# Routing stage of a two-block layer: the order on VectorE and ScalarE written out by hand, the sums of squares and the late bf16 splits moved behind the index chain, one quarter of the output projection emitted in two halves

## The chip, the cores and the metric

The kernel runs on one core of a Trainium2 chip. The metric is device time in microseconds (us) of one execution. The kernel before took 942.03 us (median of 3 runs, 939.92 to 942.48).

## The reference, cut to what matters

Two transformer blocks follow each other on 256 tokens of width 1024. The change lies at the end of the second block, where its output projection is added to the residual and the tokens are routed to 32 experts (4 groups of 8, the best group and the best 2 of its experts):

```python
mix = jnp.concatenate([y_a, y_b], axis=-1)
x = x + jnp.einsum('bse,ed->bsd', mix, w_out[l])
h = rmsnorm(x, ffn_norm[l]).reshape(B * S, D)
...
group_logits = jnp.einsum('td,dg->tg', h, w_group)
g_sel = jnp.argmax(group_logits, axis=-1)
expert_logits = jnp.einsum('td,de->te', h, w_router)
...
in_prob = jax.nn.softmax(in_group, axis=-1)
top_p, top_i = lax.top_k(in_prob, EXPERT_TOPK)
...
hid = silu(h @ w_gate[e]) * (h @ w_up[e]) * combine[..., e]
y = y + hid @ w_down[e]
```

## The kernel before, in words

**Projection.** The output projection `w_out_2` is the generator `tm_steps`. It runs over four quarters of the inner dimension in the order `WO = [0, 2, 1, 3]`, and each quarter multiplies two token tiles `t` by two column halves `c` into four PSUM tiles `ps_wo` (`acc[t][c]`). Every product is three matmuls (high by high, low by high, high by low). The weights of the last quarter are split ahead of time into the tiles `hph` and `hpl`; its 24 matmuls (4 tiles x 2 inner steps x 3) come last, tile after tile. The generator is advanced by `next(wo)`, and `step` advances the attention work that is emitted between.

**Routing.** `route` handles four blocks `(t, c)` of 128 tokens by 512 columns. For each block VectorE adds the projection to the residual (`w<-w,ps_wo`), TensorE transposes the sum (four `ps_acc<-ident,w`), VectorE or ScalarE (ACT) copies the transposed block to `h3T`, and TensorE makes the router logits from it (`ps_acc<-wgr,h3T`). Each block is also split into three bf16 parts in the tiles `h3` (rows name them `h`): ACT rounds the sum (`h<-w`), VectorE takes the remainder (`r_rem<-w,h`), ACT rounds that (`h<-r_rem`), VectorE takes the last remainder (`h<-r_rem,h`). ACT also makes the sum of squares of each block (`r_ss`) for the norm. From the logits VectorE makes the choice of experts in some twenty small instructions (from `rm` to `rM`), TensorE counts positions with a triangular matrix (`lt`), VectorE writes `posm`, and from it the 0/1 matrices `Gm` that gather the tokens of four experts. The norm factors (`r_sm`, `r`) come from a chain of tiny VectorE instructions over `r_ss`.

**Experts.** `experts` then runs on TensorE in an order written out by hand: the gather (`ps_acc<-Gm,h`, 24 short matmuls for the first half), the copies `xg` out of PSUM by ACT and VectorE in turns, the up products (`ps_acc<-w,xg`), the down products (`ps_acc<-w,mhT`) and the scatter into `ps_wo` (`Y`). Weights stream in through a ring of 1 MB tiles `w` from the SP queue; a load waits until its tile has been given free. One of these tiles is the residual itself (`w_87` when numbered), free once routing has read it.

**What sets the order.** Each engine runs its own queue in order. In `route` the order on every engine is found by a list scheduler, with a priority offset (`high_priority(offset=RP[t])`) for the adds, transposes and copies; TensorE is by hand only in `experts`. Small temporaries of `route` live in a pool that is closed before `experts` opens its own pool in the same memory.

Of the kernel before, what the change touches and what calls it, by code (L numbers as in the profile page):

```python
# [6 lines left out]
F32 = mybir.dt.float32  # L7
# [62 lines left out]
MP = 2  # L70
MS = {mybir.EngineType.DVE, mybir.EngineType.Activation, mybir.EngineType.PE}
# [21 lines left out]
class K:  # L93
# [362 lines left out]
    def tm_steps(self, src, x, nk, xt=(), tag="acc", pre=(), order=None, each=None):  # L456
# [13 lines left out]
        for n, r in enumerate(order):  # L470
# [9 lines left out]
            for t in range(2):  # L480
                for k, w in now:
                    for c in range(2):
                        mms(k, t, c, w)
                    if each:
                        each()
            yield acc
# [1096 lines left out]
    def block2(self):  # L1583
# [170 lines left out]
        wo = self.tm_steps(a["w_out_2"], mx, 8, xt, "wo", [self.tload(a["w_out_2"], r) for r in WO], WO, lambda: step(NW))  # L1754
        more = True
        for n, r in enumerate(WO):
# [16 lines left out]
            if n < 3:  # L1773
                next(wo)
                step(NS)
        for self.acc2 in wo:
            pass
# [14 lines left out]
    def route(self, big, wgr):  # L1792
# [8 lines left out]
        self.rs3, sums = [], []  # L1801
        CS = [slice(c * 512, (c + 1) * 512) for c in range(2)]
        for t in range(2):
            ts = slice(t * 128, (t + 1) * 128)
            h = self.hres[t]
            ss = pool.tile([128, 2], F32, name="r_ss", bufs=2)
            sums.append(ss)
            with self.tc.high_priority(offset=RP[t]):
                for c in range(2):
                    self.tt(h[:, CS[c]], h[:, CS[c]], acc[t][c], OP.add)  # L1810
                    p = self.ps("acc")
                    for k in range(4):
                        self.tr(p[:, k * 128:(k + 1) * 128], h[:, (4 * c + k) * 128:(4 * c + k + 1) * 128])
                    dst, src = hT[:, 4 * c:4 * c + 4, ts], p.rearrange("p (a b) -> p a b", a=4)
                    V.tensor_copy(dst, src) if RE[2 * t + c] else self.cpa(dst, src)
            with self.tc.high_priority(offset=RQ[t]):
                for k in range(8):
                    self.mm(lg[:, t], hT[:, k, ts], wgr[:, k, :], k == 0, k == 7)
            self.dump_rows("x2", t, h)
        for t in range(2):  # L1820
            for c in range(2):
                self.act(h3[2][:, t, CS[c]], self.hres[t][:, CS[c]], AF.Square, accum_out=sums[t][:, c:c + 1])
        for t in range(2):
            for c in range(2):
                src = self.hres[t][:, c * 512:(c + 1) * 512].rearrange("q (p k) -> q k p", k=8)
                b = [x[:, t].rearrange("q (k p) -> q k p", k=8)[:, :, 64 * c:64 * c + 64] for x in h3]
                r = big.tile([128, 8, 64], F32, name="r_rem", bufs=2)
                e1, e2 = [(V, self.G)[x] for x in SE[4 * t + 2 * c:4 * t + 2 * c + 2]]
                self.cpa(b[0], src)
                self.tt(r, src, b[0], OP.subtract, eng=e1)  # L1830
                self.cpa(b[1], r)
                self.tt(b[2], r, b[1], OP.subtract, eng=e2)
        self.Y = [[self.ps("wo") for _ in range(2)] for _ in range(2)]
        for t in range(2):
            for c in range(2):
                self.mm(self.Y[t][c], self.ident, self.hres[t][:, CS[c]], True, False)
# [17 lines left out]
        o1 = first_max(el, m1, "r1", [4, 8], more8)  # L1854
        in2 = mb("rin2", 4, 8)
        self.stt(in2, o1, -3.0e38, el, OP.mult, OP.add)
        first_max(gl, gm, "rg", [4], more4[:, :8], ohg)
        ogb = ohg[:, :, :, None].to_broadcast([128, 2, 4, 8])
# [308 lines left out]
```

## Time and profile before

| | before |
|---|---|
| median of 3 runs | 942.03 us |
| profiled execution, its own time | 944.24 us |
| span of that execution, first to last instruction | 942.5 us |
| TensorE busy, and mean granted clock | 885.3 us (94%), 0.961 of full speed |
| VectorE (DVE), ACT, GpSimd (POOL) busy | 596.3, 413.3, 48.1 us |
| weights and data moved | 197.56 MB, mean 210 GB/s |

The profiled execution took 1.7 us more than its span, and 2.2 us more than the median of the runs. Busy shares are means over stages; the stage of the change is 679 to 700 us from the span's start, and the experts take the time from there on. A busy TensorE is not one at its peak, since ends of matmuls are modelled.

### The profile page before, as it was taken

What the parts mean: (1) busy time and instruction counts of PE and PEld (TensorE: products, weight loads), DVE (VectorE), ACT (ScalarE), POOL (GpSimd) and SP (SyncE); (2) the same over time, 40 slices, a digit from 0 to 9 for tenths busy, and PEclk for the clock granted to TensorE, in tenths of its full rate; (3) what the DMA queues carried; (4) which work ended last, traced back from release to release, by engine and by line L of the source; (5) the groups of instructions that cost most, each with busy time, mean ns of one, the idle gap of its engine ahead of it and who ended that gap; (6) DMA issues with size and microseconds to landing.
All of it is one profiled execution on the core that took longest, in us unless ns stands there. A gap on an engine that the chain in (4) does not pass through costs nothing.

```text
span 942.5 us, 15955 instructions
## 1 busy us (share of the span) xinstructions
PE 885.3 (94%) x6204; PEld 671.2 (71%) x6204; DVE 596.3 (63%) x1477; ACT 413.3 (44%) x807; POOL 48.1 (5%) x73
## 2 busy tenths in 40 slices
PE   7986989999999999999998999999989999999983
PEld 6986867689999899998877998886654443444421
DVE  6698699979888667665578788666473222323214
ACT  4373335376855246654452456576452111222102
POOL 2000232111000000000000010000000000000001
PEclk7898789999999999999999999999999999999997
DMA  6624222134696356646772543334969999999971
GB/s 186 186 69 142 82 90 90 57 123 136 199 293 216 97 180 181 188 170 229 254 234 87 179 134 109 117 134 145 388 239 347 374 396 398 410 404 408 406 258 48
DMA packets 111028, 197.56 MB, mean 210 GB/s; under 512 B 13161, under 2 KB 77906, under 8 KB 110946
## 3 DMA queue, kind: packets, MB, share of 16 engines
q1 hardware_dynamic: 110658, 195.95, 60.1%
q8 instruction: 51, 0.84, 0.4%
q10 hardware_dynamic: 288, 0.52, 0.1%
q14 instruction: 31, 0.25, 0.1%
HBM read 195.40 MB, written 1.05 MB: 208 GB/s over the span
## 4 chain that ended last, share of the span: by engine, by line
PE 72%; DVE 15%; ACT 6%; DMA 4%; issue 2%; POOL 0%; SPq 0%; DVEq 0%; ACTq 0%
PE ps_acc L132 41%; PE ps_mm L132 25%; PE ps_wo L132 4%; DVE wlo L139 3%; PE ps_acc L136 2%; ACT whi L154 2%; DMA w<-in_w_up_dram 2%; DVE cv_y L148 1%; DVE s5z L807 1%; DMA w<-in_w_down_dram 1%; DVE s5z L139 1%; ACT mo_P L151 1%; DMA ln_g<-in_ln_g_dram 1%; DVE r L148 1%; DMA w<-in_w_in_dram 1%
## 5 line engine op out<-in xcount | busy, mean ns | idle before, releaser
L139 DVE TENSOR_TENSOR wlo<-w,whi 128x1024 fp32r<-128x1024 f32 x150 | 185.6, 1240 | 77.6 <-ACT whi L154 76.7
L154 ACT ACTIVATE whi<-w 128x1024 fp32r<-128x1024 f32 x150 | 158.2, 1058 | 167.0 <-PE ps_mm L132 110.1
L132 PE MATMUL ps_mm<-hph,whi 128*128 128x256 f32 x424 | 122.7, 289 | 0.0
L132 PE MATMUL ps_mm<-hph,wlo 128*128 128x256 f32 x424 | 121.3, 286 | 0.0
L132 PE MATMUL ps_mm<-hpl,whi 128*128 128x256 f32 x424 | 121.0, 285 | 0.0
L132 PE MATMUL ps_acc<-w,xg 128*64 128x512 f32 x512 | 117.0, 597 | 0.0
L132 PE MATMUL ps_mm<-hTh,wlo 128*128 128x256 f32 (+1 forms) x360 | 107.0, 297 | 7.2 <-DVE pre L866 6.2
L132 PE MATMUL ps_mm<-hTh,whi 128*128 128x256 f32 (+1 forms) x360 | 108.8, 303 | 0.7 <-ACT gth L151 0.4
L132 PE MATMUL ps_mm<-hTl,whi 128*128 128x256 f32 (+1 forms) x360 | 106.2, 295 | 0.0
L132 PEld LDWEIGHTS ps_acc<-w,xg 128*64 128x64 f32 x512 | 35.2, 137 | 67.7 <-issue 62.5
L132 PEld LDWEIGHTS ps_mm<-hph,whi 128*128 128x128 f32 x424 | 80.5, 190 | 1.8 <-issue 1.8
L132 PEld LDWEIGHTS ps_mm<-hph,wlo 128*128 128x128 f32 x424 | 80.4, 190 | 1.2 <-issue 1.2
L132 PEld LDWEIGHTS ps_mm<-hpl,whi 128*128 128x128 f32 x424 | 80.5, 190 | 0.6 <-issue 0.6
L132 PEld LDWEIGHTS ps_mm<-hTh,wlo 128*128 128x128 f32 x360 | 72.0, 200 | 8.5 <-DVE pre L866 6.4
L132 PEld LDWEIGHTS ps_mm<-hTh,whi 128*128 128x128 f32 x360 | 72.1, 201 | 6.0 <-issue 2.6
L132 PEld LDWEIGHTS ps_mm<-hTl,whi 128*128 128x128 f32 x360 | 71.8, 200 | 0.8 <-issue 0.7
L132 PE MATMUL ps_acc<-w,mhT 128*32 128x512 f32 x512 | 59.4, 594 | 1.0 <-DVE mhT L1991 1.0
L151 ACT ACTIVATE mth<-ps_acc,cb 128x256 f32<-128x256 f32 x16 | 7.6, 474 | 119.8 <-PE ps_acc L132 119.8
L148 DVE SCALAR_TENSOR_TENSOR mth<-mth,ps_acc 128x256 f32<-128x256 f32 x16 | 6.7, 420 | 82.5 <-ACT mth L151 82.5
L139 DVE TENSOR_TENSOR hpl<-ps_acc,hph 128x512 fp32r<-128x512 f32 x40 | 26.0, 685 | 49.8 <-ACT hph L154 49.8
L154 ACT ACTIVATE hph<-ps_acc 128x512 fp32r<-128x512 f32 (+1 forms) x44 | 23.7, 576 | 62.6 <-PE ps_acc L132 61.7
L132 PEld LDWEIGHTS ps_acc<-w,mhT 128*32 128x32 f32 x512 | 19.6, 110 | 34.3 <-issue 30.0
(605 smaller groups left out, 1732.5 us busy)
## 6 DMA issues: line engine op xcount, KB each, us to landing
w<-in_w_down_dram SPq DMA_DIRECT2D x46, 1024.0 KB, 6.7
w<-in_w_in_dram SPq DMA_DIRECT2D x36, 1024.0 KB, 5.3
w<-in_w_gate_dram SPq DMA_DIRECT2D x60, 512.0 KB, 10.9
w<-in_w_up_dram SPq DMA_DIRECT2D x60, 512.0 KB, 10.0
w<-in_w_up_dram SPq DMA_DIRECT2D x16, 1024.0 KB, 5.8
w<-in_m_w_out_dram SPq DMA_DIRECT2D x4, 1024.0 KB, 5.6
w<-in_s_w_glu_dram SPq DMA_DIRECT2D x8, 512.0 KB, 5.8
w<-in_w_o_dram SPq DMA_DIRECT2D x4, 1024.0 KB
```

The source lines that it names most:

```text
L132: self.PE.matmul(out, lhsT, rhs, start=start, stop=stop, **kw)
L136: self.PE.transpose(out, in_, self.ident[:n, :n])
L139: (eng or self.V).tensor_tensor(out, a, b, op)
L148: (eng or self.V).scalar_tensor_tensor(out, a, s, b, op0, op1, **kw)
L151: self.S.activation(out, in_, func, bias=bias, scale=scale, **kw)
L154: self.S.activation(out, in_, AF.Copy)
L807: self.V.tensor_tensor_scan(flat(z[:, i]), d, flat(z[:, i]), 0.0, OP.mult, OP.add)
```

## The change

`tm_steps` gets a parameter `mid`: in quarter number 2 it yields once more after the first token tile, and the caller takes one more `next`. In `route` the loops over the blocks are replaced by a sequence of calls inside `manual_schedule(engines=RM)`, which holds the written order on VectorE and ACT (TensorE is still ordered by the scheduler). The priorities are gone. Per block there are now `add` (add and transposes), `logits`, `first`, `second` and `third` (the steps of the split). The sums of squares stand last and write their unused output to `hT` (rows: `h3T`) instead of `h3`.

```diff
+RM = {mybir.EngineType.DVE, mybir.EngineType.Activation}
...
+                if n == mid and t == 0:
+                    yield acc
...
-            with self.tc.high_priority(offset=RP[t]):
-                for c in range(2):
-                    self.tt(h[:, CS[c]], h[:, CS[c]], acc[t][c], OP.add)
-                    p = self.ps("acc")
-                    for k in range(4):
-                        self.tr(p[:, k * 128:(k + 1) * 128], h[:, (4 * c + k) * 128:(4 * c + k + 1) * 128])
...
-        for t in range(2):
-            for c in range(2):
-                self.act(h3[2][:, t, CS[c]], self.hres[t][:, CS[c]], AF.Square, accum_out=sums[t][:, c:c + 1])
...
+        def first(t, c):
+            src, b = part(t, c)
+            self.cpa(b[0], src)
+
+        def second(t, c):
+            src, b = part(t, c)
+            rem[t, c] = r = big.tile([128, 8, 64], F32, name="r_rem", bufs=2)
+            self.tt(r, src, b[0], OP.subtract)
+            self.cpa(b[1], r)
+
+        def third(t, c):
+            src, b = part(t, c)
+            self.tt(b[2], rem[t, c], b[1], OP.subtract)
...
+        with self.tc.manual_schedule(engines=RM):
+            dst, src = add(0, 0)
+            first(0, 0)
+            V.tensor_copy(dst, src)
+            logits(0, 0)
+            dst, src = add(0, 1)
+            second(0, 0)
+            self.cpa(dst, src)
+            logits(0, 1)
+            first(0, 1)
+            dst, src = add(1, 0)
+            third(0, 0)
+            first(1, 0)
+            V.tensor_copy(dst, src)
+            logits(1, 0)
+            dst, src = add(1, 1)
+            first(1, 1)
+            second(0, 1)
+            V.tensor_copy(dst, src)
+            logits(1, 1)
+            third(0, 1)
+            second(1, 0)
...
+            self.mm(p[:, 0:64], self.lt, Mf.rearrange("p t e -> p (t e)"), True, True)
+            second(1, 1)
+            third(1, 0)
+            third(1, 1)
+            self.stt(self.posm, p[:, 0:64], 1.0, Mff.bitcast(F32), OP.add, OP.mult)
+            for t in range(2):
+                for c in range(2):
+                    self.act(hT[:, 4 * c:4 * c + 4, t * 128:(t + 1) * 128],
+                             self.hres[t][:, CS[c]].rearrange("p (a b) -> p a b", a=4), AF.Square,
+                             accum_out=sums[t][:, c:c + 1])
```

TensorE, in the last quarter of the projection, before: matmul 10 of its 24, then the transposes of the first block, then the others with the second block's transposes among them.

```order
L132 MATMUL ps_wo<-hph,mx2h 128x512
L136 MATMUL ps_acc<-ident,w 128x128 x4
L132 MATMUL ps_wo<-hpl,mx2h 128x512
L132 MATMUL ps_wo<-hph,mx2l 128x512
L132 MATMUL ps_wo<-hph,mx2h 128x512
L132 MATMUL ps_wo<-hpl,mx2h 128x512
L132 MATMUL ps_wo<-hph,mx2l 128x512
L132 MATMUL ps_wo<-hph,mx2h 128x512
L132 MATMUL ps_wo<-hpl,mx2h 128x512
L136 MATMUL ps_acc<-ident,w 128x128 x4
```

The same engine after: the last of the 24 projection matmuls, and what follows it.

```order
L133 MATMUL ps_wo<-hph,mx2l 128x512
L137 MATMUL ps_acc<-ident,w 128x128 x4
L133 MATMUL ps_wo<-w,ident 128x512
L133 MATMUL ps_acc<-wgr,h3T 128x36 x4
L137 MATMUL ps_acc<-ident,w 128x128 x4
L133 MATMUL ps_wo<-w,ident 128x512
L137 MATMUL ps_acc<-ident,w 128x128 x3
L133 MATMUL ps_acc<-wgr,h3T 128x36 x4
L137 MATMUL ps_acc<-ident,w 128x128
```

All transposes have moved behind the 24 matmuls, and the logits of each block stand between them; the three transposes of the third block are parted from the fourth by the logits of the second.

ACT in `route`, before: the squares are the rows that write `r_ss`.

```order
L151 ACTIVATE h_7679,r_ss<-w 128x512
L154 ACTIVATE h_7679<-w 128x8x64
L151 ACTIVATE h_7679,r_ss<-w 128x512
L154 ACTIVATE h_7679<-r_rem 128x8x64
L154 ACTIVATE h3T<-ps_acc 128x4x128
L154 ACTIVATE h_7679<-w 128x8x64
L151 ACTIVATE h_7679,r_ss<-w 128x512
L154 ACTIVATE h_7679<-w 128x8x64
L151 ACTIVATE h_7679,r_ss<-w 128x512
```

ACT at the same place after, up to the first exponentials of the router (`re`).

```order
L155 ACTIVATE h_7679<-w 128x8x64
L155 ACTIVATE h_7679<-r_rem 128x8x64
L155 ACTIVATE h3T<-ps_acc 128x4x128
L155 ACTIVATE h_7679<-w 128x8x64 x3
L155 ACTIVATE h_7679<-r_rem 128x8x64 x3
L152 ACTIVATE h3T,r_ss<-w 128x4x128 x4
L152 ACTIVATE re_7850<-re_7850,r_7824 128x4
```

The four squares have moved behind all eight roundings.

VectorE from the end of the choice (`rM`) to the first `Gm`, after, with the engines that each row waits for (before, seven rows stand between `rM` and `Gm`, `posm` and small ones, none of them longer than 128x64 elements and none waiting for ACT).

```order
L140 TENSOR_TENSOR rM<-ro_7786,ro_7787 128x64 [waits DVE_49]
L140 TENSOR_TENSOR r_rem<-w,h_7679 128x512
L140 TENSOR_TENSOR h_7679<-r_rem,h_7679 128x8x64 [waits Activation_49] x2
L149 SCALAR_TENSOR_TENSOR posm<-ps_acc,rM 128x64 [waits PE_49]
L140 TENSOR_TENSOR r_sm<-r_ss 128x1 [waits Activation_49]
...
L149 SCALAR_TENSOR_TENSOR r_7824<-r_7825,r_7824 128x1 [waits DVE_49]
L140 TENSOR_TENSOR Gm<-iota_343,posm 128x128 [waits Activation_49]
```

One remainder and two last remainders now stand between `rM` and `posm`, and `Gm` waits for ACT, since its memory lies in the closed pool that the squares write; the sum `r_sm` of the second token tile, a few rows later, has no wait of its own.

## Rows read from the trace of the kernel before

**Rows 1.** The page, part 4: shares of the span in the chain of work that ended last, by engine.

```profile
PE 72%; DVE 15%; ACT 6%; DMA 4%; issue 2%; POOL 0%; SPq 0%; DVEq 0%; ACTq 0%
```

**Rows 2.** The chain that ended last, in order of time, from the last projection quarter on: start in us from the span's start, length, engine, tile written, line, count.

```profile
679.49 4.01 PE ps_wo L132 x10
...
684.14 0.50 DVE h3T L1815
...
687.62 1.05 ACT h L154
...
691.41 2.07 ACT h L154 x3
693.50 1.08 DVE r_rem L139
...
698.60 0.22 DVE posm L148
...
699.23 16.31 PE ps_acc L132 x109
...
897.49 1.13 PE ps_wo L132 x4
```

**Rows 3.** The list of waits from 690 to 942 (who waited for whom: us in total, times, longest), and one stretch of the experts from the view by stretches (busy us of PE, PEld, DVE, ACT and POOL with their counts, granted clock, mean share of the DMA engines, GB/s).

```profile
PEld ps_acc L132 <- DMA w<-in_w_up_dram: 0.7, 3, 0.3
...
PEld ps_acc L132 <- DMA w<-in_w_gate_dram: 0.3, 1, 0.3
...
740.00:760.00 20.00, 20.00 (x167) 8.87 (x165) 6.57 (x19) 4.93 (x10) 0.00 (x0) 1.00 1.02 407
```

**Rows 4.** The timeline of the last projection quarter: start us, us, engine, line, operation, out<-in, count, in brackets the idle time before and who ended it.

```profile
681.83 0.69 DVE L139 TENSOR_TENSOR w<-w,ps_wo 128x512 f32<-128x512 f32 x1 [1.54 <-PE ps_wo L132]
...
682.87 0.63 PE L132 MATMUL ps_wo<-hph,mx2h 128*128 128x512 f32 x1
...
683.30 0.80 PE L136 MATMUL ps_acc<-ident,w 128*128 128x128 f32 x4
...
684.40 0.39 PE L132 MATMUL ps_wo<-hph,mx2h 128*128 128x512 f32 x1
...
684.63 0.39 PE L132 MATMUL ps_wo<-hpl,mx2h 128*128 128x512 f32 x1
...
684.75 0.68 DVE L139 TENSOR_TENSOR w<-w,ps_wo 128x512 f32<-128x512 f32 x1
...
685.34 1.13 DVE L139 TENSOR_TENSOR r_rem<-w,h 128x512 f32<-128x512 f32 x1
...
685.55 0.60 PE L136 MATMUL ps_acc<-ident,w 128*128 128x128 f32 x4
```

**Rows 5.** The timeline further on: a square with the read of its accumulator and the rounding behind it, the copy to `h3T` on ACT, a second rounding, two last remainders on VectorE.

```profile
688.55 0.64 ACT L151 ACTIVATE h<-w 128x512 bf16<-128x512 f32 x1
...
689.08 0.21 ACT L151 ACTIVATION_READ_ACCUMULATOR h<-w 128x1 f32 x1
...
689.17 1.15 ACT L154 ACTIVATE h<-w 128x512 bf16<-128x512 f32 x1
...
690.80 0.61 ACT L154 ACTIVATE h3T<-ps_acc 128x512 f32<-128x512 f32 x1
...
691.80 0.65 ACT L154 ACTIVATE h<-r_rem 128x512 bf16<-128x512 f32 x1
...
691.96 1.29 DVE L139 TENSOR_TENSOR h<-r_rem,h 128x512 bf16<-128x512 f32 x2 [0.21 <-ACT h L154]
```

**Rows 6.** The timeline of the choice of experts: the last logits matmuls, the last matmuls ahead of the choice, its first two instructions and its last.

```profile
691.74 1.17 PE L132 MATMUL ps_acc<-wgr,h3T 128*128 128x36 f32 x9
...
692.74 2.82 PE L132 MATMUL ps_wo<-w,ident 128*128 128x512 f32 x6
...
694.50 0.21 DVE L1843 TENSOR_REDUCE rm<-ps_acc 128x8 f32<-128x64 f32 x1
...
694.76 0.21 DVE L139 TENSOR_TENSOR r_eq<-ps_acc,rm 128x64 f32<-128x64 f32 x1
...
697.93 0.22 DVE L139 TENSOR_TENSOR rM<-ro,ro 128x64 fp32r<-128x64 f32 x1
```

**Rows 7.** The timeline at the first up products: the first copy `xg` by VectorE, and the weight load that waited for it.

```profile
701.13 0.48 DVE L143 TENSOR_SCALAR xg<-ps_acc,gperm 128x256 f32<-128x256 f32 x1
...
701.66 0.19 PEld L132 LDWEIGHTS ps_acc<-w,xg 128*64 128x64 f32 x2 [0.76 <-DVE xg L143]
```

**Rows 8.** An early idle stretch of TensorE, first the timeline's row of the matmul that ended it, then slices of one us from the view by stretches (columns as in rows 3, the granted clock third from the end) for it and for the idle stretch ahead of the gather.

```profile
81.19 0.60 PE L132 MATMUL ps_mm<-hTh,wlo 128*128 128x272 f32 x1 [6.17 <-DVE pre L866]
...
80.00:81.00 1.00, 0.00 (x0) 0.00 (x0) 1.00 (x2) 0.00 (x0) 0.00 (x0) 0.50 0.00 0
...
86.00:87.00 1.00, 1.00 (x9) 1.00 (x8) 0.62 (x2) 0.64 (x1) 0.00 (x0) 0.81 0.00 0
...
697.00:698.00 1.00, 0.00 (x0) 0.00 (x0) 1.00 (x10) 0.00 (x0) 0.00 (x0) 1.00 1.04 426
```

**Rows 9.** The timeline of the SP queue: the two loads into the residual's memory, and the four `w_down` loads behind them.

```profile
693.88 0.33 SPq L392 DMA_DIRECT2D w<-in_w_gate_dram  x1
695.59 0.33 SPq L392 DMA_DIRECT2D w<-in_w_up_dram  x1
704.48 8.02 SPq L395 DMA_DIRECT2D w<-in_w_down_dram  x4
```

More of the change, by code (lines that the diff above doesn't have):

```diff
@@ L1753, in block2 @@
         ready = (lambda: mdone[0] >= 2, lambda: mdone[0] >= 4, lambda: done[0], lambda: done[1])
[L1754 removed]
+        wo = self.tm_steps(a["w_out_2"], mx, 8, xt, "wo", [self.tload(a["w_out_2"], r) for r in WO], WO, lambda: step(NW), 2)
         more = True
@@ L1775, in block2 @@
                 step(NS)
+            else:
+                next(wo)
         for self.acc2 in wo:
@@ L1800, in route, with add @@
             self.G.memset(m[:, :, 0:1], 0.0)
-        self.rs3, sums = [], []
+        self.rs3 = []
         CS = [slice(c * 512, (c + 1) * 512) for c in range(2)]
-        for t in range(2):
-            ts = slice(t * 128, (t + 1) * 128)
+        def add(t, c):
             h = self.hres[t]
-            ss = pool.tile([128, 2], F32, name="r_ss", bufs=2)
-            sums.append(ss)
-            with self.tc.high_priority(offset=RP[t]):
-                for c in range(2):
-                    self.tt(h[:, CS[c]], h[:, CS[c]], acc[t][c], OP.add)
-                    p = self.ps("acc")
-                    for k in range(4):
-                        self.tr(p[:, k * 128:(k + 1) * 128], h[:, (4 * c + k) * 128:(4 * c + k + 1) * 128])
[L1814 to L1819, printed above, removed]
@@ L1820, in route @@
-        for t in range(2):
-            for c in range(2):
-                self.act(h3[2][:, t, CS[c]], self.hres[t][:, CS[c]], AF.Square, accum_out=sums[t][:, c:c + 1])
[L1823 to L1832, printed above, removed]
+            self.tt(h[:, CS[c]], h[:, CS[c]], acc[t][c], OP.add)
@@ new lines, in add, with logits, part @@
+            p = self.ps("acc")
+            for k in range(4):
+                self.tr(p[:, k * 128:(k + 1) * 128], h[:, (4 * c + k) * 128:(4 * c + k + 1) * 128])
+            return hT[:, 4 * c:4 * c + 4, t * 128:(t + 1) * 128], p.rearrange("p (a b) -> p a b", a=4)
+        def logits(t, c):
+            for k in range(4 * c, 4 * c + 4):
+                self.mm(lg[:, t], hT[:, k, t * 128:(t + 1) * 128], wgr[:, k, :], k == 0, k == 7)
+        def part(t, c):
+            src = self.hres[t][:, c * 512:(c + 1) * 512].rearrange("q (p k) -> q k p", k=8)
+            b = [x[:, t].rearrange("q (k p) -> q k p", k=8)[:, :, 64 * c:64 * c + 64] for x in h3]
+            return src, b
@@ new lines, in route @@
+        rem = {}
+        def first(t, c):
[9 more added lines that the diff above has]
+            self.tt(b[2], rem[t, c], b[1], OP.subtract)
+        sums = [pool.tile([128, 2], F32, name="r_ss", bufs=2) for _ in range(2)]
```

34 lines of the change are left out of this document (16 added, 18 removed).

## The prediction

> **What bounds the kernel now.** I read the page's chain of work first: 72% of it is TensorE [rows 1]. The chain in order of time says where. From the first gather matmul at 699.23 us it is TensorE piece after piece (16.31 us to begin with, 1.13 us at 897.49 still so); the products of the last two experts, the norm and the store follow [rows 2]. So whatever delays the first gather delays the end by as much, unless the experts stood waiting for something that arrives meanwhile. In the list of waits they hardly do: TensorE waited for weight loads 0.7 and 0.3 us in all, though the DMA engines are full (share 1.02 between 740 and 760) [rows 3].
>
> Ahead of the gather the chain runs from the last projection quarter (679.49) over the first copy to `h3T` (684.14) to ACT, which carries it with roundings and squares nearly all the way from 687.62 to 693.48; then come VectorE's last remainder (693.50), the choice of experts, and `posm` at 698.60 [rows 2]. The change rebuilds just this stretch, so I follow it instruction by instruction: the new order, with durations and distances between starts from the timeline.
>
> **The projection in two halves.** Up to matmul 10 of the last quarter the rows of every engine stand in the same order before and after, those of quarter three too. It moves no instruction, so I cost it at nothing, and it needs no cover.
>
> **Transposes behind the projection.** Matmul 10 starts at 682.87, the transposes of the first block at 683.30 and take 0.80 us, and VectorE copies at 684.14 [rows 2, 4]. After, 14 more matmuls stand in the way. At 0.23 us from one to the next (684.40 to 684.63) they go from 683.30 to 686.5; four transposes at full clock take 0.60 us (685.55) [rows 4], so the copy starts at 687.2, **3.05 us later**. VectorE has only the first add (681.83) to do before that. It can't pass the copy, so everything behind it waits: ten instructions up to the third remainder, then the choice. The gain on the other side is that the 24 matmuls end about 1 us earlier without eight transposes among them, but nobody waits for the last of them any more.
>
> **VectorE's queue to the first reduction.** From that copy on the queue holds 3 copies, 3 adds, 3 remainders and 2 last remainders. The next start follows 0.61 us after a copy (684.14 to 684.75), 0.60 after an add (684.75 to 685.34), 1.08 after a remainder (its duration at 693.50), 0.60 after a last remainder (two take 1.29, with a tail) [rows 2, 4, 5]. That is 3 x 0.61 + 3 x 0.60 + 3 x 1.08 + 2 x 0.60 = 8.1 us. One stall comes on top. The fourth transpose of block three now stands behind the logits of block two; these wait for ACT's copy of that block, and ACT's copy stands behind the second rounding of block one. The remainder of block one ends at 689.5; 0.65 us of rounding, 0.61 us of copy [rows 5], 0.52 us for four logits matmuls (1.17 for nine) [rows 6] and one transpose bring 691.5, where VectorE would copy at 690.75: **0.75 us**. First reduction: 687.2 + 8.1 + 0.75 = 696.05, against 694.50 [rows 6]: 1.55 us late, and I take 1.6.
>
> **The choice itself.** It ran from 694.50 to 697.93, the start of `rM` [rows 6], with a last remainder and a dozen norm instructions mixed in. These are gone, but the chain of the group choice now stands ahead of the second maximum, and each short instruction waits out its predecessor. Between 2.8 us (the 0.60 of the remainder taken out) and the 3.43 of before, I take 3.4: dependent starts are 0.26 us apart (694.50 to 694.76) [rows 6], and some thirteen of the twenty depend on the one before. `rM` starts at 699.5.
>
> **Splits and squares ahead of the gather.** Behind `rM` VectorE takes the last block's remainder (1.08 us, to 700.8), ACT rounds it (0.65 us, to 701.45) [rows 2, 5], and VectorE finishes that block before it may write `posm`. Where `posm` started 0.67 us after `rM` (698.60 after 697.93) [rows 2, 6], it now does so 2.7 us after, near 702.2. But that isn't what ends last. ACT's four squares come only now, since ACT's queue is held by that rounding: 0.62 us from one start to the next (688.55 to 689.17), 0.74 for the last with its accumulator read (689.08 + 0.21 - 688.55) [rows 5], so they end at 701.45 + 3 x 0.62 + 0.74 = 704.05. `Gm` waits for the last one, as its row tells. One `Gm` later the gather starts, at **704.4, 5.2 us after 699.23**. The norm instructions now ahead of `Gm` I cost at nothing: they run while the last two squares do. Without this cover they would cost eight starts, some 1.4 us.
>
> **Behind the gather.** TensorE's second up product waited for VectorE's `xg` (701.13, 0.48 us) until 701.66 [rows 7]. In VectorE's new queue that copy stands behind the norm chain of the second tile, which starts only with the last square: some nine tiny steps of 0.2 us and the rest of the `Gm`, so it starts near 706.8 and ends at 707.3, 5.7 us late. The fourth `xg` comes behind eight more small ones, and I give it another 0.2. **Sum so far 5.9 us**; bounds 4.5 (choice 2.8, no stall) and 6.6 (two stalls).
>
> **The clock.** TensorE now stands idle from about 695.2 to 704.4, but for one short matmul on `rM`. The rows show two cases like it. Ahead of 81.19 it had nothing to do for 6.17 us; the granted clock stood at 0.50 in the slice at 80, and came back only in the slice 86 to 87, some 5 us after work had begun. In the shorter idle stretch here before, from 695.56 (692.74 + 2.82), it stayed at 1.00 [rows 6, 8]. Nine microseconds are nearer the first. If 5 us of dense work run at half clock, half of that is lost, 2.5 us; some lies beside the waits for `xg`, so I take **1.9 us** (0 to 2.6).
> The Trainium skill, "TensorE: Matmul & The Clock Gate", Part 1, says that an idle array falls back to 1.2 GHz and that only renewed activity lifts the throttle. The slice at 80 agrees, the one at 697 shows no fall yet; by the page the sum is the one with the 1.9 us, without it the 5.9 us alone.
>
> **The residual as a weight tile.** Two loads go into the residual's memory and now wait for the squares: about 703 and 704.1 instead of 693.88 and 695.59. Behind them on SP stand the `w_down` loads, which waited until 704.48 [rows 9] for tiles that the first up products free; these move with the experts. So a shift of 8.5 us lies under 8.9 us of waiting and costs nothing. If that cover is gone, the loads are 8.5 us late where the experts are 7.8: 0.7 us at most.
>
> **Sum.** 0 + 5.9 + 1.9 = 7.8 us. On the profiled execution's own 944.24 us that is 952.0; this execution lay 2.2 us above the median of the runs, so for a median I forecast 942.0 + 7.8 = **949.8 us**. What the measurement can tell from no change is about 0.3%, 2.8 us.
>
> **Rivals.**
> *The clock stays up.* The idle stretch before shows that it can [rows 8]. Then 947.9 us (944.7 to 949). Against it: the stretch is over twice as long.
> *The weight stream pays it back.* The DMA engines are full from 740 on [rows 3]. If the experts were bound by weights, a later start would find more of them there, and the end would stay at 942 to 944. Against it: only 1.0 us of waits for weights, and a stream whose next tiles are freed by the first up products.
> *ACT was the chain, and loses 2.5 us.* Four squares (4 x 0.62) leave ACT's queue ahead of the last roundings, for which the remainder at 693.50 waited. Place: ACT from 687.62 to 693.48 [rows 2]. The logits stood ready at 692.9 (691.74 + 1.17) [rows 6], so the choice could begin 1.6 us earlier: 940.4 us. It decides if the first copy starts before about 685.6 (687.2 less the 1.6 by which the choice is late) and the squares stay out of the way of `Gm`; the orders of the queues speak against it.
>
> **How the numbers follow.** Forecast with the clock's fall 0.64, its own range 947.5 to 952.5; clock up 0.22; paid back 0.10; faster 0.04. The range leaves out the last two and a little at its ends: 945.2 to 953.0. Slower by over 0.3% (above 944.9): the first two but 0.01, so 0.85; within 0.3%: 0.11; faster: 0.04.
>
> **What the profile after would show.** Right: all 24 projection matmuls before the first transpose; the first copy to `h3T` 7.7 us after the quarter's first matmul (4.65 before); four squares on ACT in a row behind an idle stretch, and `Gm` within 0.3 us of their end; the first gather 25 us after the quarter's first matmul (19.74 before); the clock at half when it starts; the experts' pieces as long as before. Wrong: `Gm` ahead of the last square, up products that wait for weights, or a choice that starts no later than 15.0 us after the quarter's first matmul.

## The result, and the profile after

The changed kernel took 947.43 us (median of 12 runs, 944.67 to 953.12), the kernel before on the same chip 942.97 us (933.44 to 944.58): 4.5 us by the medians, and a ratio of 1.0064 with a 95% interval of 1.0042 to 1.0087, which is 6.0 us. It is slower, by less than the 7.8 us forecast; 947.43 lies in the range of 945.2 to 953.0 and just below the likeliest case's own (947.5 to 952.5). A second comparison on another occasion (run e5) gave 1.0069 (1.0043 to 1.0095).

The page after: span, busy time, and the shares of the chain that ended last. TensorE's share was 72% before [rows 1]. Its busy time is shorter by 1.4 us and the span longer by 2.7, so what was lost is time in which it stood: 4.1 us more of it (61.3 after 57.2).

```profile
span 945.2 us, 15956 instructions
...
PE 883.9 (94%) x6204; PEld 670.7 (71%) x6204; DVE 598.9 (63%) x1478; ACT 413.0 (44%) x806; POOL 48.1 (5%) x73
...
PE 73%; DVE 15%; ACT 6%; DMA 3%; issue 2%; POOL 0%; SPq 0%; DVEq 0%; ACTq 0%
```

The timeline of the changed kernel from the last matmul of the quarter to the first up product (start, length, engine, line, operation, tiles, count, in brackets the wait and who ended it), to be held against [rows 4 to 7].

```profile
682.57 0.39 PE L133 MATMUL ps_wo<-hph,mx2l 128*128 128x512 f32 x1
682.81 0.60 PE L137 MATMUL ps_acc<-ident,w 128*128 128x128 f32 x4
683.44 0.69 DVE L1867 COPY h3T<-ps_acc 128x512 f32<-128x512 f32 x1 [3.94 <-PE ps_acc L137]
...
688.19 0.69 DVE L1877 COPY h3T<-ps_acc 128x512 f32<-128x512 f32 x1 [1.07 <-PE ps_acc L137]
...
692.80 0.21 DVE L1849 TENSOR_REDUCE rm<-ps_acc 128x8 f32<-128x64 f32 x1
...
696.38 0.22 DVE L140 TENSOR_TENSOR rM<-ro,ro 128x64 fp32r<-128x64 f32 x1
...
697.63 0.63 ACT L155 ACTIVATE h<-r_rem 128x512 bf16<-128x512 f32 x1 [4.09 <-DVE r_rem L140]
...
698.90 0.22 DVE L149 SCALAR_TENSOR_TENSOR posm<-ps_acc,rM 128x64 f32<-128x64 f32 x1
...
699.52 0.16 DVE L140 TENSOR_TENSOR r_sm<-r_ss 128x1 f32<-128x1 f32 x1 [0.40 <-ACT h3T L152]
...
700.52 0.19 ACT L152 ACTIVATION_READ_ACCUMULATOR h3T<-w 128x1 f32 x1
700.87 0.48 DVE L140 TENSOR_TENSOR Gm<-iota,posm 128x128 bf16<-128x128 f32 x2
...
701.29 2.72 PE L133 MATMUL ps_acc<-Gm,h 128*128 128x128 bf16 x24 [4.15 <-DVE Gm L140]
...
702.83 0.47 ACT L152 ACTIVATE xg<-ps_acc,gperm 128x256 f32<-128x256 f32 x1 [0.49 <-PE ps_acc L133]
...
703.43 0.48 DVE L144 TENSOR_SCALAR xg<-ps_acc,gperm 128x256 f32<-128x256 f32 x1
...
703.94 0.65 PE L133 MATMUL ps_acc<-w,xg 128*64 128x512 f32 x1
```

VectorE waits 3.94 us for the first copy, because all 24 matmuls now stand ahead of the transposes; ACT waits 4.09 us in the middle and then has its four squares to do; `Gm` follows the last square's accumulator read by 0.16 us (700.71 to 700.87). TensorE is idle from 692.35 to 701.29 but for the matmul on `rM`, and the view by stretches (granted clock third from the end) shows what became of its clock, where it had stayed at 1.00 before [rows 8]:

```profile
693.00:694.00 1.00, 0.00 (x0) 0.00 (x0) 0.79 (x5) 0.54 (x1) 0.00 (x0) 0.88 0.75 307
694.00:695.00 1.00, 0.00 (x0) 0.00 (x0) 0.90 (x7) 0.00 (x0) 0.00 (x0) 0.50 0.13 53
...
703.00:704.00 1.00, 1.00 (x11) 0.81 (x8) 0.93 (x6) 0.76 (x3) 0.00 (x0) 0.50 0.68 197
704.00:705.00 1.00, 1.00 (x4) 0.42 (x4) 0.89 (x7) 0.50 (x2) 0.00 (x0) 1.00 0.32 131
```

**How traces are compared here.** The quarter's first matmul starts at other times in every execution (672 to 679 us), so I give distances from it. One more thing moves: the granted clock falls to half for some 3 us at places that differ from one execution to the next. Experiments e11 and e12 are the same program; in e11 the fall lay in the quarter, in e12 not, and everything behind it up to the first up product is 1.50 us apart (gather at 19.45 and 17.95). A second fall in e11, from 693 to 697, makes the second part of the gather 2.80 us apart. The changed kernel's profile has no such fall, that of before has one. So 1.5 us have to be added to the changed kernel's distances before they are held against those of before.

| run | first copy to `h3T` | first reduction | `rM` | `posm` | gather | first up product | second part of gather | fall in the quarter | ratio to before (95%) |
|---|---|---|---|---|---|---|---|---|---|
| before | 4.65 | 15.01 | 18.44 | 19.11 | 19.74 | 21.23 | 26.67 | yes | |
| changed | 6.32 | 15.68 | 19.26 | 21.78 | 24.17 | 26.82 | 32.21 | no | 1.0064 (1.0042 to 1.0087) |
| e1 | 6.33 | 15.69 | 19.33 | 21.86 | 22.55 | 25.20 | 31.34 | no | 1.0056 (1.0034 to 1.0078) |
| e2 | 3.15 | 13.13 | 16.73 | 19.25 | 21.64 | 24.29 | 30.94 | no | 1.0068 (1.0045 to 1.0091) |
| e3 | 7.86 | 17.22 | 20.81 | 24.40 | 30.51 | 31.97 | 37.32 | yes | 1.0092 (1.0072 to 1.0113) |
| e4 | 4.62 | 15.00 | 18.43 | 19.10 | 19.73 | 21.52 | 28.17 | yes | 0.9995 (0.9975 to 1.0014) |
| e5 | 6.31 | 15.68 | 19.28 | 21.80 | 24.20 | 26.85 | 32.25 | no | 1.0069 (1.0043 to 1.0095) |
| e6 | 7.86 | 17.23 | 20.82 | 23.34 | 25.73 | 27.19 | 32.54 | yes | 1.0039 (1.0018 to 1.0059) |
| e7 | 3.14 | 13.12 | 16.77 | 19.31 | 20.00 | 22.64 | 28.38 | no | 1.0030 (1.0012 to 1.0047) |
| e8 | 4.61 | 14.59 | 18.25 | 20.77 | 21.46 | 22.92 | 28.27 | yes | 1.0006 (0.9988 to 1.0023) |
| e9 | 7.88 | 18.78 | 22.38 | 24.91 | 27.31 | 29.27 | 35.72 | yes | 1.0063 (1.0040 to 1.0086) |
| e10 | 4.63 | 14.06 | 17.72 | 20.25 | 20.95 | 22.41 | 27.76 | yes | 1.0006 (0.9982 to 1.0031) |
| e11 | 4.63 | 15.14 | 18.17 | 18.84 | 19.45 | 21.22 | 27.99 | yes | 0.9975 (0.9954 to 0.9996) |
| e12 | 3.13 | 13.64 | 16.67 | 17.34 | 17.95 | 19.72 | 25.19 | no | 0.9984 (0.9966 to 1.0001) |

Distances are us from the quarter's first matmul in each run's profiled execution. With the 1.5 us the changed kernel is behind before by 3.2 at the first copy, 2.2 at the first reduction, 4.2 at `posm`, 5.9 at the gather and 7.1 at the first up product.

### The profile page after: what moved, and what is told of

Its sections match the earlier page's. It is cut to its first block, busy times and chain, and to the rows that moved or that the text cites. A ratio compares the mean times of both kernels' runs of the same rounds, so it can differ in the third digit from the quotient of the medians.

```text
span 945.2 us, 15956 instructions
## 1 busy us (share of the span) xinstructions
PE 883.9 (94%) x6204; PEld 670.7 (71%) x6204; DVE 598.9 (63%) x1478; ACT 413.0 (44%) x806; POOL 48.1 (5%) x73
## 4 chain that ended last, share of the span: by engine, by line
PE 73%; DVE 15%; ACT 6%; DMA 3%; issue 2%; POOL 0%; SPq 0%; DVEq 0%; ACTq 0%
PE ps_acc L133 42%; PE ps_mm L133 24%; PE ps_wo L133 4%; DVE wlo L140 3%; PE ps_acc L137 3%; ACT whi L155 2%; DMA w<-in_w_up_dram 2%; DVE cv_y L149 1%; DVE s5z L810 1%; DVE s5z L140 1%; DMA ln_g<-in_ln_g_dram 1%; ACT mo_P L152 1%; DVE r L149 1%; DVE rot L140 1%; DMA w<-in_w_in_dram 1%
```

## Experiments

**Squares in ACT's gap (e1), transposes first (e2), both (e7).** The first takes the squares from the end into the stretch where ACT waits, the second gives the transposes back the priority they had.

```diff
             second(1, 0)
+            for t in range(2):
+                for c in range(2):
+                    self.act(hT[:, 4 * c:4 * c + 4, t * 128:(t + 1) * 128],
+                             self.hres[t][:, CS[c]].rearrange("p (a b) -> p a b", a=4), AF.Square,
+                             accum_out=sums[t][:, c:c + 1])
```
```diff
+            with self.tc.high_priority(offset=RP[t]):
                 for k in range(4):
                     self.tr(p[:, k * 128:(k + 1) * 128], h[:, (4 * c + k) * 128:(4 * c + k + 1) * 128])
```

> The changed kernel with one thing altered: ACT's four squares stand behind the rounding of the third block's remainder, in the stretch where ACT waited 4.09 us (693.5 to 697.6 in the changed kernel's trace), and no longer behind the last rounding. Theory (the squares hold Gm, and the norm chain holds the first xg on VectorE): the squares run from 693.5 to 696.0, nobody waits for them, eight norm instructions slip into the choice and cost it 0 to 0.4 us; Gm follows posm within 0.3 us, the gather starts 1.4 us nearer to the quarter's first matmul (22.8 instead of 24.17 us) and the first up product 1.3 us nearer (25.5 instead of 26.8). Time 1.3 us below the changed kernel, 946.1 us, ratio to the kernel before 1.0050. Rival (the squares only filled a wait that the last remainder and its rounding impose anyway): Gm stays where it is, ratio 1.0064. Rival (the norm chain inside the choice costs as much as it saved, 8 starts of 0.2 us, 1.6 us): rM later by 1.6 us, ratio 1.0064 or above.

> The changed kernel with the priority of before given back to the four transposes of each block, and nothing else: the first block's transposes stand behind matmul 10 again, the other rows of VectorE and ACT as in the changed kernel. Theory (the transposes behind the 24 matmuls made the first copy to h3T 3.05 us late, 1.4 to 1.7 without the clock's fall in the quarter): the first copy starts 4.6 us after the quarter's first matmul at half clock or 3.3 at full clock (6.32 in the changed kernel), VectorE's queue of some 8.1 us and one stall of 0.7 us follow, the first reduction starts 13.5 us after the quarter's first matmul (15.68 in the changed kernel). All behind it comes 2.2 us earlier: 945.2 us, ratio to the kernel before 1.0040. Rival (VectorE's queue is paced by ACT's roundings or TensorE's later transposes): the earlier first copy is waited away before the third block, the reduction comes less than 0.7 us earlier, ratio 1.0058 to 1.0064.

> The changed kernel with the squares in ACT's gap and the transposes with their priority of before, both together. Theory (the two parts add up on VectorE's queue): first reduction 13.1 us after the quarter's first matmul, rM 16.8, posm 19.4, the gather 20.0 (24.17 in the changed kernel, 19.74 in the one before), at half clock with the first up product 2.65 us behind it, 22.7 (26.82 and 21.23); the clock's return costs up to 1.3 us more behind it. Ratio to the kernel before 1.0015 to 1.003, 3 to 4.5 us below the changed kernel. Rival (the two overlap, because either moves the same wait): the gather at 21.5 or later, ratio above 1.004.

In e1 the gather came 1.62 us nearer, `Gm` 0.26 us behind `posm`, and `rM` stood still. That is the squares' share, and the rivals are out. In e2 the first copy came 3.17 us earlier, the first reduction 2.55, the gather 2.53. In e7 both together gave 4.17 us, nearly the sum (1.62 + 2.53 = 4.15): two delays in one queue, one behind the other. By the ratio only e7 differs: 1.0030 against 1.0069 for the changed kernel in the same comparison (e5), 3.1 us by the medians, though the intervals still overlap a little. For e1 the ratio settles nothing; its interval, some 2 us to either side, contains both the changed kernel's ratio and the expected one. For e2 the forecast of the time missed: the interval contains the changed kernel's ratio and leaves out the expected 1.0040. Of its 2.5 us half was lost again by the second part of the gather (30.94 against 32.21), and that the rest reached the end isn't shown.

Part of the gain was given back behind the gather, as the timeline of e1 shows in its first up products: they take 6.21 us where the changed kernel takes 5.46.

```profile
694.95 2.72 PE L133 MATMUL ps_acc<-Gm,h 128*128 128x128 bf16 x24 [2.47 <-DVE Gm L140]
...
697.00 0.48 DVE L144 TENSOR_SCALAR xg<-ps_acc,gperm 128x256 f32<-128x256 f32 x1 [0.34 <-ACT xg L152]
...
697.60 6.21 PE L133 MATMUL ps_acc<-w,xg 128*64 128x512 f32 x16
```

The stretches say why: in e1 the clock is back only in the slice at 699, by its mean of 0.89 some 4.3 us after the gather's start, and in e2 in the slice at 701, 5.3 us after, where the changed kernel had it back after 2.7. First the slice of e1, then that of e2:

```profile
699.00:700.00 1.00, 1.00 (x3) 0.27 (x2) 0.90 (x6) 0.00 (x0) 0.00 (x0) 0.89 0.00 0
...
701.00:702.00 1.00, 1.00 (x2) 0.16 (x1) 0.29 (x1) 0.28 (x1) 0.00 (x0) 0.69 0.02 8
```

The timeline's row of `xg` in e1 has VectorE waiting (0.34 us); its norm chain no longer stands in front. Yet the up product starts 2.65 us behind the gather's start, exactly as in the changed kernel. So the half-clock gather alone is enough to hold it that long. The Trainium skill, "TensorE: Matmul & The Clock Gate", Part 1, has two rates in its table of states, half and full; the rows agree, 0.50 and 1.00, and 0.89 and 0.69 are slices in which the rate changed.

**The halves alone (e4).**

```diff
+                if n == mid and t == 0:
+                    yield acc
```

> The kernel before with one part of the change alone: the last quarter of the projection emitted in two halves. Theory (it moves no instruction on any engine, so it costs nothing): ratio 1.000, its interval holding 1; the run is also a measure of what such a comparison can tell from no change. Rival (emitting it in halves costs by itself, through waits that the orders of the queues do not show): over 1.002.

0.9995, and every distance up to the gather within 0.03 us of before: nothing, as costed. Its profile also shows how much chance does: the clock fell at 694, in the gather and the first up products (6.72 us), and at 916 in the last products of the experts, which makes the execution 2.8 us longer from the quarter on than the profiled one of before.

**Filler on TensorE (e3, e6), and the changed kernel again beside it (e5).**

```diff
+            fl = self.ps("acc")
+            for _ in range(3):
+                self.mm(fl, self.ident, rem[1, 0].rearrange("p a b -> p (a b)"), True, True)
```

The same stands behind the matmul on `rM` with `rem[1, 1]`; e3 has 7 and 8 in place of 3 and 3.

> The changed kernel with work added that no result uses: seven matmuls 128x512 on TensorE between the last logits and the matmul on rM, and eight between that and the gather, into a PSUM tile of their own, so that TensorE is busy in most of the stretch where it stood idle (692.35 to 701.29) and the granted clock may stay up. Theory A (the fall of the clock costs what the gather takes longer, 2.72 less 1.53 us): the gather runs 24 matmuls in 1.5 us at clock 1.00 and the first up product starts 1.2 us earlier; 946.2 us, ratio to the kernel before 1.0051. Theory B (VectorE reaches the first xg only at the end of its norm chain, 2.14 us after the gather's start, whatever the gather does): the gather is as short, yet the first up product starts no more than 0.2 us earlier, ratio 1.0062 to 1.0064. Theory C (the filler does not keep the clock): the gather stays at 2.7 us, ratio 1.0064 or, if the filler delays the matmul on rM, up to 1.007.

> The changed kernel itself once more, on the chip that also runs the next three, so that they can be held against it and not only against the kernel before. Theory (the loss is the gather, 4.43 us later by distance from the quarter's first matmul, 24.17 against 19.74, and a half-clock stretch of which the profiled execution hid a part): ratio to the kernel before 1.005 to 1.008; in the profile the gather again 24.2 us after the quarter's first matmul, or 25.7 with a fall of the clock in the quarter, and the granted clock at 0.50 when it starts. If the clock comes back about 5 us after the gather's start, as in the two experiments with moved squares and moved transposes, and not 2.7 us as in the first profile, the second part of the gather starts 33 us after the quarter's first matmul, not 32.2. Rival (the first comparison was mostly chance of the clock elsewhere): ratio below 1.003.

> The changed kernel with three unused 128x512 matmuls (two passes of 0.43 us each) between the last logits and the matmul on rM and three more behind it; they fit into the stretch where TensorE stood idle, so that rM's matmul is not held up. Theory A (the half clock at the gather costs 1.2 us and more behind it): granted clock 1.00 from 694 on, gather in 1.5 us, the first up product 1.2 us earlier, ratio 0.0015 to 0.002 below that of the changed kernel in the same call. Theory B (VectorE's norm chain holds xg, so the gather's length does not show until the up products): the first up product starts where it did, 26.8 us after the quarter's first matmul, and only what the up products lost to a late return of the clock is won, 0 to 1 us; ratio 0 to 0.001 below. Theory C (the pauses between the pieces let the clock fall all the same): gather 2.7 us, no difference.

I had sized e3 wrongly: such a matmul is two records of 0.43 us, not one, so the first seven ran for 6.25 us, past `rM` (698.65), and held its matmul up until 700.97. The kernel is slower, 1.0092, but it shows that the clock can be kept: the granted clock is 1.00 from 682, the end of the quarter's fall, to behind the gather, which takes 1.50 us. e5 repeats the changed kernel within 0.04 us at every distance of the table; the clock came back in the slice at 702 (0.95), again 2.7 us after the gather began, and not the 5 us that I had supposed. e6 fits into the idle stretch, as its timeline of TensorE shows:

```profile
696.20 0.27 PE L133 MATMUL ps_acc<-rM,lt 128*128 128x64 f32 x1 [0.92 <-DVE rM L140]
697.19 2.81 PE L133 MATMUL ps_acc<-r_rem,ident 128*128 128x512 f32 x6 [0.72 <-DVE r_rem L140]
700.74 1.50 PE L133 MATMUL ps_acc<-Gm,h 128*128 128x128 bf16 x24 [0.74 <-DVE Gm L140]
702.20 5.42 PE L133 MATMUL ps_acc<-w,xg 128*64 128x512 f32 x16
```

and the stretches of e6 have the clock at 1.00 where the gather starts:

```profile
700.00:701.00 1.00, 0.26 (x6) 0.29 (x6) 0.97 (x7) 0.15 (x2) 0.00 (x0) 1.00 0.67 225
```

The gather is short, the first up product stands 1.46 us behind its start instead of 2.65, and the ratio falls from 1.0069 to 1.0039 (medians 947.48 and 945.75 us; the intervals overlap, so the ratio alone doesn't prove it). Useless work on TensorE brought the first up product 1.2 us nearer, with the fall in the quarter taken out (27.19 less 1.5, against 26.85). Between theory A and theory B the rows decide. The timeline of VectorE in e6 has its first `xg`:

```profile
702.24 0.48 DVE L144 TENSOR_SCALAR xg<-ps_acc,gperm 128x256 f32<-128x256 f32 x1
```

The first up product stands at 702.20, ahead of it, so it can't have waited for it. It reads ACT's copy; what VectorE copies is read from the second product on, as [rows 7] tell for before. That the scheduler also moved three norm steps of e6 behind this `xg` (now 1.93 us behind `Gm` instead of 2.56) thus doesn't touch the first up product. In the changed kernel ACT's copy was ready at 703.30 and the gather ended at 704.01: there too the first up product followed the gather, and the clock alone made it 1.2 us late. VectorE's copy, ready at 703.91, came in time for the second product, whose weights the timeline has at 704.43, without a wait for `xg`:

```profile
704.43 0.14 PEld L133 LDWEIGHTS ps_acc<-w,xg 128*64 128x64 f32 x1 [0.29 <-DVE rw L149]
```

**Both parts undone, with filler (e8).** As e7, with two and one unused matmuls.

> The one before this with three unused matmuls added on TensorE, two between the last residual products and the matmul on rM, one behind that, so that the idle stretch ahead of the gather is broken up. Theory (what then still parts it from the kernel before is the clock): clock 1.00, gather 20.0 us after the quarter's first matmul in 1.5 us, first up product 21.6 (21.23 before); ratio to the kernel before 1.000 to 1.001. Rival (the clock falls all the same): as the kernel without the filler, 1.0015 to 1.003.

1.0006 against 1.0030 for e7 (the intervals overlap), and level with the kernel before. With the fall in the quarter taken out of e8 its first up product is 1.2 us nearer and the second part of the gather 1.6: what the clock cost e7. Of the stretch itself 1.7 us are left (gather 21.46 against 19.74, both with a fall in the quarter). They are the remainder and the last remainders behind `rM`: `posm` starts 2.5 us after `rM`, 0.67 before.

**Residual products late (e9), and the best order by hand (e10).**

```diff
+        with self.tc.manual_schedule(engines=MS):
             logits(1, 1)
...
+            for c in range(2):
+                self.mm(self.Y[0][c], self.ident, self.hres[0][:, CS[c]], True, False)
             o1 = first_max(el, m1, "r1", [4, 8], more8)
...
+            for c in range(2):
+                self.mm(self.Y[1][c], self.ident, self.hres[1][:, CS[c]], True, False)
             second(1, 1)
```

> The changed kernel with TensorE's last logits, the four residual products and the matmul on rM written out by hand too: two residual products stand between the last logits and the matmul on rM and two behind it, where three had stood among the transposes. Nothing is added; the idle stretch is filled with work that was there. On VectorE one of the norm steps (0.2 us) moves behind the first xg, the rest stays. Theory A (the clock): granted clock 1.00 up to the gather, gather 1.5 us, the first up product 1.5 us behind the gather's start (2.65 in the changed kernel); with the transposes freed of the products VectorE's wait ahead of the second block's copy shrinks by 0.5 us or more, so the first up product comes 1.5 to 2 us earlier; ratio to the kernel before 1.004 to 1.005, 1.5 to 2.5 us below the changed kernel. Theory B (VectorE's norm chain ahead of xg is what holds the up products): gather as short, yet the first up product 2.4 us behind the gather's start, ratio 1.005 to 1.006. Rival (the products don't keep the clock): gather 2.7 us, ratio 1.006.

> The changed kernel with three edits: squares in ACT's gap, transposes with their priority of before, residual products late as in the run ahead of this; and the third block's remainder ahead of the second block's last remainder on VectorE. Theory (VectorE's two waits for transposes, 0.55 and 1.16 us in the kernel with both parts undone, shrink by about 0.9 us, and the clock stays up without unused work): first reduction 12.2 us after the quarter's first matmul, 13.7 with a fall of the clock in the quarter; gather 19.1 or 20.6, first up product 20.6 or 22.0 (21.23 before, with such a fall). Ratio to the kernel before 0.999 to 1.001. Rival (the remainder behind rM keeps it late whatever else is done): gather 20.0 or 21.5 as with both parts undone, ratio 1.001 to 1.003.

e9 missed. The idle stretch was filled, but the clock fell earlier: with the products gone from among the transposes, TensorE stood for most of two slices (0.31 and 0.27 busy), and from 683 to 693 the clock was at half, as the stretches of e9 show. It was back when the gather began and fell again inside it, at 700, so the gather took 2.03 us. That the short pauses brought the first of these falls is likely, but one execution doesn't show it.

```profile
680.00:681.00 1.00, 0.31 (x3) 0.31 (x3) 1.00 (x2) 0.00 (x0) 0.00 (x0) 1.00 0.48 115
...
682.00:683.00 1.00, 0.27 (x4) 0.06 (x2) 0.90 (x3) 0.74 (x2) 0.00 (x0) 1.00 0.98 344
683.00:684.00 1.00, 1.00 (x6) 1.00 (x7) 0.63 (x2) 1.00 (x2) 0.00 (x0) 0.55 1.09 295
```

That is just where VectorE waits for transposes, in the timeline of e9:

```profile
687.01 1.09 PE L137 MATMUL ps_acc<-ident,w 128*128 128x128 f32 x4
...
688.15 0.69 DVE L1882 COPY h3T<-ps_acc 128x512 f32<-128x512 f32 x1 [1.85 <-PE ps_acc L137]
```

Four transposes take 1.09 us, VectorE's wait grows to 1.85 us, the reduction comes 1.6 us later than in e6, and the ratio is 1.0063: no gain. e10 has the transposes first and the squares in the gap as well, and on VectorE the third block's remainder ahead of the second block's last remainder. Its clock fell for some 3 us at 689 and was back before the gather (1.50 us). Its reduction came 0.5 us earlier than in e8, not the 0.9 expected, the gather 0.5, and the ratio is 1.0006, level with before. By hand this order gets back to the kernel before and not past it.

**The squares alone (e11, e12).** The kernel before with the squares emitted behind the splits and written into `h3T`; the scheduler then puts two of them behind ACT's last roundings.

```diff
-                self.act(h3[2][:, t, CS[c]], self.hres[t][:, CS[c]], AF.Square, accum_out=sums[t][:, c:c + 1])
...
         self.Y = [[self.ps("wo") for _ in range(2)] for _ in range(2)]
...
+                self.act(hT[:, 4 * c:4 * c + 4, t * 128:(t + 1) * 128],
+                         self.hres[t][:, CS[c]].rearrange("p (a b) -> p a b", a=4), AF.Square,
+                         accum_out=sums[t][:, c:c + 1])
```

> The kernel before with one part of the change alone: the four squares are emitted behind the splits and write into h3T's memory; the scheduler then puts two of them behind ACT's last roundings, into the choice. Theory (ACT's roundings and squares were the chain from 687.62 to 693.48, so two squares less shorten it by 2 x 0.62 us): the first reduction starts 13.8 us after the quarter's first matmul (15.01), the gather 18.5 (19.74), ratio to the kernel before 0.9985 to 0.999. Rival (VectorE's queue and the logits set the reduction, ACT had slack): reduction within 0.3 us of 15.01, ratio 1.000. Rival (Gm waits for the last square, as in the changed kernel): reduction early, yet gather at 19.7 or later, ratio 1.000 or above.

> The kernel before with the squares alone moved, as in the run ahead of this, timed once more, because its profile and its ratio disagree: by the profile the gather starts 19.45 us after the quarter's first matmul against 19.74 before, 0.3 us, while the ratio was 0.9975 (0.9954 to 0.9996), some 2 us. Theory (0.3 us is all, the rest is the scatter of the runs): ratio 0.998 to 1.001, gather again 19.4 to 19.5 us after the quarter's first matmul. Rival (a gain of 2 us that the stretch itself does not show): ratio 0.9975 or less again.

The first reduction stayed where it was (15.14 against 15.01), though two squares of 0.62 us had left ACT's queue. The timeline of e11 shows what is late next: VectorE, in the order that the scheduler found, now has two last remainders ahead of the reduction, to 687.83, and the last logits of TensorE, behind two residual products, end at 687.93.

```profile
686.01 1.10 PE L132 MATMUL ps_wo<-w,ident 128*128 128x512 f32 x2
686.54 1.29 DVE L139 TENSOR_TENSOR h<-r_rem,h 128x512 bf16<-128x512 f32 x2
...
686.95 0.98 PE L132 MATMUL ps_acc<-wgr,h3T 128*128 128x36 f32 x8
...
687.96 0.22 DVE L1845 TENSOR_REDUCE rm<-ps_acc 128x8 f32<-128x64 f32 x1
```

With one remainder less in it the choice is 0.4 us shorter (3.03 against 3.43), and that is what reaches the gather. `Gm` doesn't wait for the squares, which end in the choice. Both ratios lie below 1 (0.9975 and 0.9984), the second with 1 inside its interval. The stretch shows 0.3 us at the gather (19.45 against 19.74) and nothing behind it: the first up product stands at 21.22 against 21.23, because it waited for ACT's `xg` (0.24 us in e12, below), and the second part of the gather in e12, with 1.5 us added, at 26.69 against 26.67.

```profile
699.10 5.54 PE L132 MATMUL ps_acc<-w,xg 128*64 128x512 f32 x16 [0.24 <-ACT xg L151]
```

Whether the 1 to 2 us of the ratios are real, and from where, stays open; the profiles don't show them.

## Why the prediction was right or wrong, point by point

**The projection in two halves: 0.** Right; the orders are the same, e4 measured it.

**First copy 3.05 us later.** Right. I had reckoned with a fall of the clock in the quarter, as before had it, and put the copy at 7.7 us; with such a fall it stands at 7.86 (e3, e6), and e2 took back 3.17. The profiled execution without a fall has 6.32.

**VectorE's queue 8.1 and a stall of 0.75.** Right in kind, short in size: from the first copy to the reduction 9.36 us passed, 0.5 more than 8.85. The stall measured 1.07, in the row at 688.19 and for the reason given, the fourth transpose behind the logits. So the reduction is 2.2 us late where I had 1.6: this is the larger of the two terms that were sized too small.

**The choice: 3.4.** It took 3.58 (692.80 to 696.38).

**Splits and squares ahead of the gather: +5.2.** The squares came as described, after a rounding that waited 4.09 us, and `Gm` 0.16 us behind the last. The gather is 5.9 us late where I had 5.2, by the two sizes just named. One step differs: I had `Gm` wait for the last square and the norm steps ahead of it hide beneath the squares. The chain that ended last, in order of time, leaves the squares after the second one and goes over the first tile's norm steps:

```profile
698.17 1.33 ACT h3T L152 x4
699.52 0.17 DVE r_sm L140
...
700.95 0.21 DVE Gm L140
```

The last of these steps ended at 700.95, the last square at 700.71, and VectorE has no wait in front of `Gm`. So the norm steps held it by a hair, and the wait for the last square would have held it nearly as long. e1 moved the squares and with them the norm steps; what either is worth alone isn't measured.

**`xg` behind the norm chain (the step from 5.2 to 5.9) and the clock (+1.9).** This is where the sum failed. The fall of the clock came as forecast, from 694 on, and made the gather 2.72 us instead of 1.5: 1.2 us at the first up product, where I had 1.9. The norm chain did hold VectorE's `xg`, but that cost nothing: the copy was ready at 703.91, 0.5 us before the second product's weights were loaded, so the 0.7 us lay beneath the slow gather and the first product. One price, then: 1.2 us, not 0.7 + 1.9. The 5 us for which I let the half clock run, taken from the row at 86 [rows 8], are near what e1 and e2 had (4.3 and 5.3) and too long for the changed kernel itself, where it was back after 2.7 us, in e5 too.

**The residual as a weight tile: 0.** Right. The timeline of the SP queue after, which answers to [rows 9]:

```profile
699.51 0.33 SPq L393 DMA_DIRECT2D w<-in_w_gate_dram  x1
700.74 0.33 SPq L393 DMA_DIRECT2D w<-in_w_up_dram  x1
707.63 2.18 SPq L396 DMA_DIRECT2D w<-in_w_down_dram  x2
```

By the distance from the quarter's first matmul the two loads came 8.0 and 7.5 us later and `w_down` 5.5 (1.5 more each with equal clocks), and no weight came late. The list of waits from 692 on has these for DMA in the experts (us in total, times, longest), 0.8 us in all after 1.0 [rows 3]:

```profile
PEld ps_acc L133 <- DMA w<-in_w_up_dram: 0.3, 1, 0.3
PEld ps_acc L133 <- DMA w<-in_w_down_dram: 0.3, 1, 0.3
PEld ps_acc L133 <- DMA w<-in_w_gate_dram: 0.2, 1, 0.2
```

**The sum.** 3.2 us of late copy, of which VectorE's queue made 2.2, 0.1 in the choice, 1.9 from the remainder behind `rM`, 1.7 from squares and norm chain, 1.2 from the clock: 7.1 us at the first up product with equal clocks in the quarter, where I forecast 7.8. At the end of the execution it is 6.6. As profiled it is 5.6 (26.82 less 21.23) and 5.1 at the end; the runs say 4.5 by the medians and 6.0 by the ratio, whose interval reaches from 4.0 to 8.2. What part of the runs of either kernel has a fall in the quarter isn't recorded, so the step from 7.1 to these can't be settled. That 7.1 lies so near 7.8 is in part luck: the terms up to the gather were 0.7 us too small, those behind it 1.4 too large.

**The rivals.** The clock did not stay up. The weight stream paid next to nothing back: from the second part of the gather to the end the changed kernel took 235.9 us, the one before 236.3. That ACT was the chain and its relief a gain: the condition that I had put to it, a first copy less than 6.1 us after the quarter's first matmul (685.6 less 679.49), failed with 7.8; and where no transposes stood in the way (e11, e12) two squares less brought 0.3 us at the gather and none at the first up product, because VectorE and the logits were as late as ACT.

## What to carry to other kernels

An engine's queue written by hand needs its producers in the same order: here VectorE and ACT were fixed by hand while TensorE, having lost its priorities, put the transposes behind fourteen matmuls that nobody waited for, and the fixed queue could not go around the hole. Work is not off the path because its result is wanted late: the squares moved "behind the chain" held the chain, since the norm steps that need their sums stood ahead of `Gm` in VectorE's queue, and `Gm`'s own wait, for the last of them, would have ended hardly earlier. A delay is priced at its first reader: VectorE's late `xg` cost nothing, since its reader came later still.

## What the runs showed of the hardware

The granted clock is a price of waiting that the waits do not list. A pause of TensorE from 692.35 to 701.29 with one short matmul in it brought 0.50 from 694 on. Six unused matmuls in the same pause kept 1.00 and a gather of 1.50 us instead of 2.72, with a ratio lower by 0.003 (e6 against e5, with intervals that overlap). In e9 the fall followed two slices in which TensorE was 0.31 and 0.27 busy. How late the clock comes back varies: 2.7 us after the gather began in the changed kernel and e5, 3.5 in e7, 4.3 in e1, 5.3 in e2. Short falls at changing places cost 1.2 to 1.8 us each: 1.5 in the quarter (e11 against e12), 1.3 in the first up products (the same two), 1.2 to 1.8 in the last products of the experts (e12 against before, e2 against the changed kernel). So one profile of a kernel can be over 2 us off another of the same program: from the quarter to the end e11 took 265.5 us and e12 262.8.
